# A hybrid decoder layer: gates spread over all partitions, sums of x and fourth-operand passes on POOL, attention weights merged ahead of the transpose

## The chip, the cores and the metric

The kernel runs on one core of one Trainium2 chip. The core's engines are TensorE (PE, with its weight loads as PEld), VectorE (DVE), ScalarE (ACT), GpSimd (POOL) and SyncE (SP, which here only issues DMAs). The metric is the device time of one launch in microseconds; the kernel before takes 2483.4 us, the median of three runs (2482.44 to 2484.32).

## The reference

One inference step of one layer: a projection of x (512 prompt rows and 8 x 4 sample rows, 2048 wide) to thirteen parts, an mLSTM branch and a sliding-window attention branch in parallel, a gated merge, an output projection and a layer norm. Everything is float32. What bears on the change:

```python
u = jnp.einsum('btd,dc->btc', x, w_in)          # parts: q_m k_m v_m o_m z_m q_a k_a v_a z_a g_m g_a i_pre f_pre
ig = i_pre + b_igate
lf = jax.nn.log_sigmoid(f_pre + b_fgate)         # 4 heads x 544 rows
...
dist = qi + WINDOW - kj                          # a block of 128 queries sees its own 128 keys and the 128 before
valid = (dist >= 0) & (dist < WINDOW) & ((blk > 0) | (kj >= WINDOW))
s = q @ k * hd ** -0.5 - slope[h] * dist         # 32 heads of 64, 4 key/value heads
p = softmax(concat([where(valid, s, -inf), sink]))[..., :-1]
out = p @ v
br_a = out * silu(z_a)
```

With a window of 128, a query at place i of its block sees the keys up to i in its own block and those beyond i in the block before: the two 128x128 blocks of weights are non-zero in opposite triangles (the own block with the diagonal).

## The kernel before

**Products.** Every product is made of three: operands are split into a high and a low part in fp32r (`hilo`, L243 to L245: ACT copies the high part, DVE subtracts it for the low part), and wh·xh, wh·xl and wl·xh are summed on PE. Weights come in by SP's DMAs as `raw` tiles of 128x1024, ACT casts `wh` (L200) and DVE subtracts for `wl` (L201).

**Seven products for eight.** The main part of the input projection takes two column tiles at a time (`paired`, L698, with `prepare`, `half_product` and `gather` from L638): a 2x2 split of weights and rows is multiplied with seven half products in place of eight. For this, sums of weight quarters are formed (L645 on DVE, or L643 as an accumulating DMA from POOL's queue), and four sums of x in tiles of 272 rows: `s1`, `n2`, `n3` and `s4`, each as a high and a low quad. `s1r`, `n2r` and `n3r` are their plain forms. A half product is 24 matmuls of 128x272 (L665 for the high weights, L667 for the low ones); its result goes to `ev` tiles by ACT (L683, L688), POOL (L684) and DVE (L686 to L694).

**The start.** x comes in by five DMAs on SP, PE transposes it (L321), ACT and DVE split it (L244, L245). For the first eight k tiles ACT also copies both halves out of PSUM into `n2r` and `s1r` (L328, L329, L339); for the others DVE subtracts (L333, L343); POOL forms `n3r` (L347). `x_sums` (L554 to L584) then makes the four operands: POOL subtracts for `n2r` (L557), `n3` is split first, then `s1` and `n2` behind the last piece of x, and once the plain products are done DVE makes the fourth operand in two passes for each of four chunks (L581, L582) and splits it. At the same time the two column tiles of V are multiplied (`gemm`, L595) and, between them, the gate columns (`gates_half`, L391).

**The gates.** `gates` (L394 to L522) works on rows of 4 partitions x 544: log-sigmoid of the forget gate by |f|, exp, a reciprocal (L421) and a series (to L433), then a running sum and maxima. `attn_values` (L524 on) transposes V and writes it out through `ev` tiles (a pool of three).

**Attention.** `attentions` (L856) goes through 16 pairs of heads as a generator; `tick()` after each half product takes it one step on, so its work stands in between the paired products. `attention` (L755 to L818) makes the scores of a head (L773), adds the slopes and takes the minimum on DVE (L775), exponentiates (L784) and scales by the sums (L790) on ACT; PE transposes seven blocks a head (L801, four own and three from the block before), they are split to `ph` and `pl` of 7x128 columns, and eight matmuls a head multiply them by V (L811). ACT, DVE and POOL finish `hT` (L814, L815, L817), SP stores it.

**Order.** The order of instructions on each engine is fixed when the kernel is built, by a scheduler that goes by priorities, buffers and `issue_after` constraints; on the chip each engine works through its list in order, waiting on semaphores. SP's and POOL's lists hold DMAs too, which wait in line like any instruction.

Of the kernel before, what the change touches and what calls it, by code (L numbers as in the profile page):

```python
# [74 lines left out]
def _build(tc, nc, i, o, es):  # L75
# [240 lines left out]
    for g in range(8):  # L316
        for q in range(2):
# [31 lines left out]
    t544 = pool(esG, "t544", 12)  # L349
# [44 lines left out]
    def gates(ps):  # L394
# [9 lines left out]
        ig, fg, u, u2 = row(), row(), row(), row()  # L404
        for p_, (u_, v_), (ig_, fg_) in zip(ps, *(
# [5 lines left out]
        V.tensor_scalar(fg, fg, bi[:, 1:2], None, op0=ALU.add)  # L411
        yield
        e_ = row()
        A.activation(e_, fg, AF.Abs)
        A.activation(e_, e_, AF.Exp, scale=-1.0)
# [3 lines left out]
        dd, s, s2, p, lf = row(), u, u2, row(), row()  # L419
        V.tensor_scalar(dd, e_, 2.0, None, op0=ALU.add)  # L420
        V.reciprocal(dd, dd)  # L421
        yield
        yield
        yield
        V.tensor_tensor(out=s, in0=e_, in1=dd, op=ALU.mult)
        V.tensor_tensor(out=s2, in0=s, in1=s, op=ALU.mult)
        yield
        V.tensor_scalar(p, s2, 1.0 / 15, None, op0=ALU.mult)
        for c in (13, 11, 9, 7, 5, 3):
            V.scalar_tensor_tensor(p, p, 1.0 / c, s2, op0=ALU.add, op1=ALU.mult)  # L430
            if c % 4 == 1:
                yield
        V.scalar_tensor_tensor(p, p, 1.0, s, op0=ALU.add, op1=ALU.mult)  # L433
        V.tensor_scalar(lf, fg, 0.0, None, op0=ALU.min)
        V.scalar_tensor_tensor(lf, p, -2.0, lf, op0=ALU.mult, op1=ALU.add)
        yield

        rst, c = s, s2
        V.memset(rst, 1.0)
        V.memset(rst[:, 0:SEQ:128], 0.0)  # L440
        V.memset(rst[:, SEQ:T:NTS], 0.0)
        V.tensor_tensor_scan(c, rst, lf, 0.0, ALU.mult, ALU.add)
        ap, d0 = lf, row()
        V.tensor_tensor(out=ap, in0=ig, in1=c, op=ALU.subtract)
        yield
        V.memset(d0, 0.0)
# [78 lines left out]
    def attn_values(kk, vt):  # L525
# [8 lines left out]
        vr, vs = ev(512), ev(128)  # L534
# [19 lines left out]
    def x_sums():  # L554
# [5 lines left out]
        for name, r_ in (("n3", n3r), ("s1", s1r), ("n2", n2r)):  # L560
            h_, l_ = S[name] = quad(act2, name)
            for ch in range(4):
                ks_ = two_k(ch)
                if name == "n3":
                    A.activation(h_[:, ks_], r_[:, ks_], AF.Copy, scale=-1.0)
                    V.scalar_tensor_tensor(l_[:, ks_], r_[:, ks_], -1.0, r32(h_[:, ks_]), op0=ALU.mult, op1=ALU.subtract)
                else:

                    with tc.issue_after(state["x_end"].ins):
                        hilo(r_[:, ks_], h_[:, ks_], l_[:, ks_])  # L570
                if ch % 2:
                    yield

        while not state.get("plain_done"):
            yield
        s4 = S["s4"] = quad(act, "s4")
        for ch in range(4):
            ks_ = two_k(ch)
            k0 = (ch * 2) % 4
            h12, l12 = (r32(xk2[p][ch // 2][:, k0:k0 + 2, 0:HT]) for p in range(2))  # L580
            V.tensor_tensor(out=n2r[:, ks_], in0=h12, in1=n2r[:, ks_], op=ALU.subtract)  # L581
            V.tensor_tensor(out=n2r[:, ks_], in0=n2r[:, ks_], in1=l12, op=ALU.add)  # L582
# [147 lines left out]
    def open_attention():  # L730
        for name, bufs in (("b1", 1), ("bs", 2), ("bt", 1), ("bq", 2), ("bm", 2)):
            bp[name] = pool(esB, name, bufs)

# [21 lines left out]
    def attention(k, qs, sz, kv):  # L755
# [5 lines left out]
        for a in range(2):  # L761
            nb = btile("b1", [128, 256], f"nb{a}")
# [1133 lines left out]
```

## Time and profile before

| | before |
|---|---|
| runs (median; lowest to highest) | 2483.4 us; 2482.44 to 2484.32 us |
| the profiled execution's time | 2483.67 us |
| its span | 2481.7 us |
| PE busy in the span | 2448.2 us |
| DVE, ACT, POOL busy | 1813.4, 1244.7, 372.7 us |

The profile is of one execution. Its page gives busy times, a chain of waits and groups of like instructions; the trace behind it can be asked for the time line of an engine, for the busy time in windows, for the waits of an engine with what ended them, and for groups by line and shape. Times are us from the start of the span. A name like `wl<-raw,wh` says what an instruction writes and reads.

### The profile page before, as it was taken

What the parts mean: (1) busy time and instruction counts of PE and PEld (TensorE: products, weight loads), DVE (VectorE), ACT (ScalarE), POOL (GpSimd) and SP (SyncE); (2) the same over time, 40 slices, a digit from 0 to 9 for tenths busy, and PEclk for the clock granted to TensorE, in tenths of its full rate; (3) what the DMA queues carried; (4) which work ended last, traced back from release to release, by engine and by line L of the source; (5) the groups of instructions that cost most, each with busy time, mean ns of one, the idle gap of its engine ahead of it and who ended that gap; (6) DMA issues with size and microseconds to landing.
All of it is one profiled execution on the core that took longest, in us unless ns stands there. A gap on an engine that the chain in (4) does not pass through costs nothing.

```text
span 2481.7 us, 48772 instructions
## 1 busy us (share of the span) xinstructions
PE 2448.2 (99%) x19542; PEld 2390.0 (96%) x19542; DVE 1813.4 (73%) x2785; ACT 1244.7 (50%) x2033; POOL 372.7 (15%) x376
## 2 busy tenths in 40 slices
PE   8999999999999999999999999999999999999997
PEld 8899999999999999999999999999999999999997
DVE  7867677677777777787877888887866654777667
ACT  6457677667667665353343444444633323434431
POOL 2111121111111111021111122211000000110101
PEclk9999999999999999999999999999999999999998
DMA  6676666666666655477677667587755546788776
GB/s 167 149 191 180 159 144 158 155 153 156 149 162 148 153 136 141 117 201 244 203 224 240 200 199 235 172 250 237 233 187 183 174 150 215 213 230 256 213 221 192
DMA packets 557172, 464.71 MB, mean 187 GB/s; under 512 B 45328, under 2 KB 454080, under 8 KB 556688
## 3 DMA queue, kind: packets, MB, share of 16 engines
q1 hardware_dynamic: 540048, 402.07, 54.4%
q0 software_dynamic: 15696, 57.15, 11.8%
q8 instruction: 154, 2.52, 0.4%
q10 hardware_dynamic: 1200, 2.36, 0.3%
q14 instruction: 74, 0.61, 0.1%
HBM read 319.06 MB, written 96.31 MB: 167 GB/s over the span
## 4 chain that ended last, share of the span: by engine, by line
PE 94%; DVE 2%; DMA 2%; ACT 1%; issue 0%; SPq 0%; POOL 0%; DVEq 0%; ACTq 0%; POOLq 0%
PE bank L665 45%; PE bank L667 22%; PE bank L210 13%; PE sm L1400 2%; PE bank L1212 1%; PE sm L1432 1%; PE sm L773 1%; PE sm L1445 1%; PE sm L811 1%; PE sm L210 1%; PE sm L801 1%; DMA raw<-in_w_in 1%; PE sm L1762 1%; PE sm L1217 1%; DVE wl L201 0%
## 5 line engine op out<-in xcount | busy, mean ns | idle before, releaser
L200 ACT CAST wh<-raw 128x1024 fp32r<-128x1024 f32 x632 | 661.9, 1048 | 806.6 <-PE bank L665 649.2
L201 DVE TENSOR_TENSOR wl<-raw,wh 128x1024 fp32r<-128x1024 f32 x632 | 776.4, 1230 | 229.6 <-ACT wh L200 202.8
L665 PE MATMUL bank<-xk,wh 128*128 128x272 f32 x2336 | 324.1, 289 | 1.9 <-DVE ev L690 1.9
L645 DVE TENSOR_TENSOR raw<-raw,raw 128x1024 f32<-128x1024 f32 x238 | 303.9, 1277 | 11.7 <-DMA raw<-in_w_in 3.6
L665 PEld LDWEIGHTS bank<-xk,wh 128*128 128x128 f32 x2336 | 303.1, 188 | 5.5 <-issue 2.6
L684 POOL TENSOR_TENSOR ev<-p,ev 128x272 f32<-128x272 f32 x82 | 123.8, 1509 | 638.5 <-ACT ev L683 590.5
L667 PE MATMUL bank<-xk,wl 128*128 128x272 f32 x1168 | 172.4, 288 | 0.8 <-DVE wl L201 0.8
L665 PE MATMUL bank<-s1h,wh 128*128 128x272 f32 x656 | 169.0, 291 | 0.1
L665 PE MATMUL bank<-n3h,wh 128*128 128x272 f32 x656 | 168.8, 289 | 0.1
L665 PE MATMUL bank<-s4h,wh 128*128 128x272 f32 x656 | 168.3, 290 | 0.1
L665 PE MATMUL bank<-n2h,wh 128*128 128x272 f32 x656 | 168.2, 289 | 0.0
L665 PE MATMUL bank<-n3l,wh 128*128 128x272 f32 x656 | 168.0, 287 | 0.0
L665 PE MATMUL bank<-n2l,wh 128*128 128x272 f32 x656 | 167.6, 287 | 0.0
L665 PE MATMUL bank<-s1l,wh 128*128 128x272 f32 x656 | 167.1, 287 | 0.0
L665 PE MATMUL bank<-s4l,wh 128*128 128x272 f32 x656 | 167.0, 287 | 0.0
L667 PEld LDWEIGHTS bank<-xk,wl 128*128 128x128 f32 x1168 | 156.5, 188 | 1.0 <-DVE wl L201 1.0
L665 PE MATMUL bank<-a11h,wh 128*128 128x272 f32 x584 | 150.6, 289 | 2.5 <-ACT wh L200 2.5
L665 PE MATMUL bank<-a11l,wh 128*128 128x272 f32 x584 | 149.8, 289 | 0.0
L210 PE MATMUL bank<-bh,wl 128*128 128x272 f32 x704 | 148.3, 289 | 0.0
L210 PE MATMUL bank<-bh,wh 128*128 128x272 f32 x704 | 148.1, 289 | 0.0
L210 PE MATMUL bank<-bl,wh 128*128 128x272 f32 x704 | 146.0, 288 | 0.9 <-DVE bl L245 0.9
L643 POOL DMA_DIRECT2D raw<-raw x90 | 77.8, 864 | 319.4 <-DVE sums L786 142.8
(487 smaller groups left out, 5554.9 us busy)
## 6 DMA issues: line engine op xcount, KB each, us to landing
raw<-in_w_in SPq DMA_DIRECT2D x296, 512.0 KB
raw<-raw POOLq DMA_DIRECT2D x90, 512.0 KB, 4.9
C<-in_state_mlstm_C SPq DMA_DIRECT2D x32, 1024.0 KB
out<-C SPq DMA_DIRECT2D x64, 512.0 KB
raw<-in_w_proj_a SPq DMA_DIRECT2D x32, 512.0 KB
raw<-in_w_proj_m SPq DMA_DIRECT2D x32, 512.0 KB
raw<-in_w_out SPq DMA_DIRECT2D x32, 512.0 KB
d_v<-ev SPq DMA_DIRECT2D x16, 272.0 KB
```

The costliest lines, as they stand in the source:

```text
L200: A.copy(wh[:, k:k + n], raw[:, k:k + n])
L201: state["split"] = V.tensor_tensor(out=wl[:, k:k + n], in0=raw[:, k:k + n], in1=r32(wh[:, k:k + n]), op=ALU.subtract)
L210: PE.matmul(ps[f][:, :w], a[:, kk], b(k, c, w), start=(k == 0 and n == 0), stop=(k == 15 and n == 2))
L643: G.dma_start(out=w[out][:], in_=w[b][:], accum_op=ALU.add)
L645: V.tensor_tensor(out=w[out][:], in0=w[a][:], in1=w[b][:], op=ALU.add)
L665: PE.matmul(ps, wh[:, k], x(p, k), start=(first and k == 0 and p == 0), stop=False, skip_group_check=True)
L667: state["end"] = PE.matmul(ps, wl[:, k], x(0, k), start=False, stop=(k == 7), skip_group_check=True)
L684: G.tensor_tensor(out=c22, in0=p1, in1=c11, op=ALU.subtract)
L773: PE.matmul(pp[:, c0 + w0:c0 + 256], qs[a][:, j * 128:j * 128 + 128], kx[:, k0:k0 + 256 - w0], start=(n == 0), stop=(n == 1))
L801: PE.transpose(pt[:, (m - m0_) * 128:(m - m0_) * 128 + 128], s_[:, b, 128:256] if own else s_[:, b + 1, 0:128], ident)
L811: PE.matmul(po[:, b * 128:b * 128 + n], VA[:, b], p_[:, 2 * b:2 * b + n // 128], start=(b == 0 and m == 0), stop=(b == 3 and m == 1), skip ...
L1400: PE.matmul(pp[:, 0:258], a[:, b * 128:b * 128 + 128], b_[:, b, f], start=(b == 0 and n == 0), stop=(b == 3 and n == 2))
```

## The change

It has five parts; numbers and order of PE's other work stay.

1. **Sums of x.** For the first eight k tiles the plain `n2r` and `s1r` are no longer copied out of PSUM by ACT, but added on POOL from the high and low halves after they are split, two k tiles at once. In `x_sums` all three splits stand behind the last piece of x, and `s1` comes ahead of `n3`.
2. **Fourth operand.** Its two passes for each of the four chunks go from DVE to POOL, ahead of the wait for the plain products.
3. **Gates.** The biased forget gate row (4x544) goes by a DMA to 17 columns on all partitions; the log-sigmoid is made there, and a second DMA takes it back to 4x544. Three memsets move to POOL.
4. **V's tail tile** in `attn_values` comes from the pool of gate rows (13 buffers, was 12) and no longer from `ev`.
5. **Attention weights.** After the exponentials POOL adds the block before to the own block (three blocks of four have one); ACT scales only the merged 128 columns; PE transposes four blocks a head; ACT copies them to `fh`, DVE subtracts for `fl`; then POOL from `fh` and DVE from `fl` multiply by a mask `upper` (the exponential of the triangle constant) for the own parts and subtract for the parts of the block before, into tiles `P` of 7x128 as before. Both heads' tiles are made ahead of the matmuls with V; the pool holds three of them, and one step of the generator is moved.

```diff
             if k < 8:
                 hilo(pt[:, 0:HT], a11[0][:, k], a11[1][:, k])
                 hilo(pt[:, HT:SEQ], a21[0][:, k, 0:SEQ - HT], a21[1][:, k, 0:SEQ - HT])
-                A.copy(n2r[:, k], pt[:, 0:HT])
-                A.copy(s1r[:, k, 0:SEQ - HT], pt[:, HT:SEQ])
...
                 hilo(src, *(a21[p][:, k4, SEQ - HT:HT] for p in range(2)))
-                A.copy(s1r[:, k4, SEQ - HT:HT], src)
+                for t_, (h_, l_) in ((s1r, a21), (n2r, a11)):
+                    for ch in (g - 1, g):
+                        ks_ = two_k(ch)
+                        G.tensor_tensor(out=t_[:, ks_], in0=r32(h_[:, ks_]), in1=r32(l_[:, ks_]), op=ALU.add)
...
-    t544 = pool(esG, "t544", 12)
+    t544 = pool(esG, "t544", 13)
...
+        w7 = t5(n=6 * 17)
...
-        e_ = row()
-        A.activation(e_, fg, AF.Abs)
-        A.activation(e_, e_, AF.Exp, scale=-1.0)
...
-        V.tensor_scalar(dd, e_, 2.0, None, op0=ALU.add)
-        V.reciprocal(dd, dd)
...
-        V.tensor_scalar(lf, fg, 0.0, None, op0=ALU.min)
-        V.scalar_tensor_tensor(lf, p, -2.0, lf, op0=ALU.mult, op1=ALU.add)
...
+        f7, e7, d7, s7, q7, p7 = (w7[:, n * 17:n * 17 + 17] for n in range(6))
+        nc.sync.dma_start(f7, fg)
+        yield
+        yield
+        A.activation(e7, f7, AF.Abs)
+        A.activation(e7, e7, AF.Exp, scale=-1.0)
+        yield
+        V.tensor_scalar(d7, e7, 2.0, None, op0=ALU.add)
+        V.reciprocal(d7, d7)
...
+        V.scalar_tensor_tensor(f7, p7, -2.0, f7, op0=ALU.mult, op1=ALU.add)
+        nc.sync.dma_start(lf, f7)
+        G.memset(rst, 1.0)
+        G.memset(rst[:, 0:SEQ:128], 0.0)
+        G.memset(rst[:, SEQ:T:NTS], 0.0)
...
-        vr, vs = ev(512), ev(128)
+        vr, vs = ev(512), t5(n=128)
...
-        for name, r_ in (("n3", n3r), ("s1", s1r), ("n2", n2r)):
+        for name, r_ in (("s1", s1r), ("n3", n3r), ("n2", n2r)):
...
-            V.tensor_tensor(out=n2r[:, ks_], in0=h12, in1=n2r[:, ks_], op=ALU.subtract)
-            V.tensor_tensor(out=n2r[:, ks_], in0=n2r[:, ks_], in1=l12, op=ALU.add)
+            G.tensor_tensor(out=n2r[:, ks_], in0=h12, in1=n2r[:, ks_], op=ALU.subtract)
+            G.tensor_tensor(out=n2r[:, ks_], in0=n2r[:, ks_], in1=l12, op=ALU.add)
+        while not state.get("plain_done"):
+            yield
...
-        for name, bufs in (("b1", 1), ("bs", 2), ("bt", 1), ("bq", 2), ("bm", 2)):
+        for name, bufs in (("b1", 1), ("bs", 2), ("bt", 3), ("bq", 2), ("bm", 2)):
...
+        A.activation(upper[:], cc[:, C_TRI:C_TRI + 128], AF.Exp)
...
+            G.tensor_tensor(out=s_[:, 1:4, 128:256], in0=s_[:, 1:4, 0:128], in1=s_[:, 1:4, 128:256], op=ALU.add)
...
-                sj = s_[:, j, 128 if j == 0 else 0:256]
+                sj = s_[:, j, 128:256]
                 A.activation(sj, sj, AF.Copy, scale=sums[:, j:j + 1])
...
-            ph, pl = (btile("bt", [128, 7, 128], t_, F32R) for t_ in ("ph", "pl"))
-            for m0_, m1_ in ((0, 4), (4, 7)):
-                pt = sm()
-                for m in range(m0_, m1_):
-                    b, own = m // 2, m % 2 == 0
-                    PE.transpose(pt[:, (m - m0_) * 128:(m - m0_) * 128 + 128],
-                                 s_[:, b, 128:256] if own else s_[:, b + 1, 0:128], ident)
-                n = m1_ - m0_
-                hilo(blk(pt[:, 0:n * 128], n), ph[:, m0_:m1_], pl[:, m0_:m1_])
-            yield
+            pt = sm()
+            for b in range(4):
+                PE.transpose(pt[:, b * 128:b * 128 + 128], s_[:, b, 128:256], ident)
+            fh, fl = s_[:, :, 0:128], s_[:, :, 128:256]
+            A.copy(fh.bitcast(F32R), blk(pt[:]))
+            V.tensor_tensor(out=fl.bitcast(F32R), in0=blk(pt[:]), in1=fh, op=ALU.subtract)
+            up = bp["upper"][:].unsqueeze(1).to_broadcast([128, 4, 128])
+            both = []
+            for e, f in ((G, fh), (V, fl)):
+                p_ = btile("bt", [128, 7, 128], "P", F32R)
+                e.tensor_tensor(out=p_[:, 0:7:2], in0=f, in1=up, op=ALU.mult)
+                e.tensor_tensor(out=p_[:, 1:7:2], in0=f[:, 1:4], in1=r32(p_[:, 2:7:2]), op=ALU.subtract)
+                both.append(p_)
+            ps_.append(both)
+            yield
+        for a in range(2):
             yield
             po = sm()
...
-                for m, p_ in enumerate((ph, pl)):
+                for m, p_ in enumerate(ps_[a]):
...
-        yield
+            if a == 0:
+                yield
```

More of the change, by code (lines that the diff above doesn't have):

```diff
@@ L421, in gates @@
-        V.reciprocal(dd, dd)
+        A.activation(e7, f7, AF.Abs)
[3 more added lines that the diff above has]
+        V.reciprocal(d7, d7)
+        V.tensor_tensor(out=s7, in0=e7, in1=d7, op=ALU.mult)
+        V.tensor_tensor(out=q7, in0=s7, in1=s7, op=ALU.mult)
+        V.tensor_scalar(p7, q7, 1.0 / 15, None, op0=ALU.mult)
+        for n in (13, 11, 9, 7, 5, 3):
+            V.scalar_tensor_tensor(p7, p7, 1.0 / n, q7, op0=ALU.add, op1=ALU.mult)
@@ L422, in gates @@
+        V.scalar_tensor_tensor(p7, p7, 1.0, s7, op0=ALU.add, op1=ALU.mult)
+        V.tensor_scalar(f7, f7, 0.0, None, op0=ALU.min)
+        V.scalar_tensor_tensor(f7, p7, -2.0, f7, op0=ALU.mult, op1=ALU.add)
[3 more added lines that the diff above has]
+        G.memset(rst[:, SEQ:T:NTS], 0.0)
         yield
         yield
-        yield
-        V.tensor_tensor(out=s, in0=e_, in1=dd, op=ALU.mult)
-        V.tensor_tensor(out=s2, in0=s, in1=s, op=ALU.mult)
@@ L427, in gates @@
[L427 to L433, printed above, removed]
-        V.tensor_scalar(lf, fg, 0.0, None, op0=ALU.min)
-        V.scalar_tensor_tensor(lf, p, -2.0, lf, op0=ALU.mult, op1=ALU.add)
-        yield
-        rst, c = s, s2
-        V.memset(rst, 1.0)
@@ L563, in x_sums @@
                 ks_ = two_k(ch)
[L564 to L569, printed above, removed]
+                with tc.issue_after(state["x_end"].ins):
+                    if name == "n3":
+                        A.activation(h_[:, ks_], r_[:, ks_], AF.Copy, scale=-1.0)
+                        V.scalar_tensor_tensor(l_[:, ks_], r_[:, ks_], -1.0, r32(h_[:, ks_]), op0=ALU.mult,
+                                               op1=ALU.subtract)
+                    else:
                         hilo(r_[:, ks_], h_[:, ks_], l_[:, ks_])
```

20 lines of the change are left out of this document (11 added, 9 removed).

## The prediction

> **What bounds the kernel now.** I read the page's first part and its chain of waits, then PE's waits over the whole run, then the engines' busy time in windows: ten-microsecond ones at the start, and the sixteen periods of attention (141 to 960 us). In a window row the figures after the window's length are busy us of PE, PEld, DVE, ACT and POOL, then granted clock, DMA share and GB/s; a sum row speaks for itself.
>
> ```profile
> PE 2448.2 (99%) x19542; PEld 2390.0 (96%) x19542; DVE 1813.4 (73%) x2785; ACT 1244.7 (50%) x2033; POOL 372.7 (15%) x376
> PE 94%; DVE 2%; DMA 2%; ACT 1%; issue 0%; SPq 0%; POOL 0%; DVEq 0%; ACTq 0%; POOLq 0%
> 473.00:520.00 47.00, 47.00 (x382) 47.00 (x381) 33.65 (x54) 33.01 (x61) 8.85 (x7) 1.00 0.62 151
> sum 819.00, PE 818.33 PEld 817.59 DVE 592.54 ACT 552.65 POOL 145.12; mean PE 48.14 PEld 48.09 DVE 34.86 ACT 32.51 POOL 8.54
> 10.00:20.00 10.00, 8.03 (x41) 6.99 (x42) 5.96 (x14) 7.90 (x25) 1.34 (x1) 0.83 1.09 360
> 20.00:30.00 10.00, 9.00 (x64) 7.70 (x65) 8.39 (x18) 9.25 (x30) 6.11 (x5) 1.00 0.37 38
> 30.00:40.00 10.00, 9.45 (x77) 9.24 (x77) 8.33 (x16) 6.50 (x12) 4.24 (x4) 1.00 0.66 169
> 40.00:50.00 10.00, 9.29 (x75) 9.04 (x75) 9.90 (x17) 4.17 (x10) 3.54 (x3) 1.00 0.28 72
> 50.00:60.00 10.00, 10.00 (x82) 10.00 (x82) 9.96 (x17) 6.60 (x12) 1.01 (x1) 1.00 0.69 165
> ```
>
> PE is busy for 2448.2 of 2481.7 us and holds 94% of the chain: only PE work removed, or PE idle time made or closed, moves the end. In the attention PE is full (0.67 us idle in 819), while DVE, ACT and POOL have 13, 14 and 38 us of room in a period of 47. At the start it is otherwise: PE idles 2.97 us between 10 and 30, and between 40 and 60 DVE is full (19.86 of 20). So the change has to be judged in two places with opposite limits.
>
> **Term 1: transposes in the attention.** Each of 32 heads drops from seven 128x128 transposes to four; 96 go, and the PV matmuls stay at 8 per head. PE's timeline gives the price (start, us, engine, line, operation, and in brackets the idle time before with its releaser): seven transposes, then the start of what follows them. The last row is their group, with count, busy us and mean ns.
>
> ```profile
> 483.62 0.92 PE L801 MATMUL sm<-cc,s 128*128 128x128 f32 x7
> 484.31 0.37 PE L665 MATMUL bank<-s1h,wh 128*128 128x272 f32 x1
> 491.27 0.95 PE L801 MATMUL sm<-cc,s 128*128 128x128 f32 x7
> 491.97 2.26 PE L665 MATMUL bank<-xk,wh 128*128 128x272 f32 x16
> L801 PE MATMUL sm<-cc,s 128*128 128x128 f32 x224 | 30.0, 274 | 0.0
> ```
>
> 484.31 less 483.62 is 0.69, 491.97 less 491.27 is 0.70: 0.0986 us a transpose in the stream. The group's busy time, 30.0/224 = 0.134, holds overlap with neighbours and is the upper bound. 96 x 0.0986 = 9.5 us saved (at most 12.9). I take 9.5, since starts in a full stream are what the end follows.
>
> **What must cover it.** The split tiles that PV reads are now made after the transposes from the four merged blocks, and most of that is POOL's. Per head: an add of 128x3x128 ahead of the transposes, a product 128x4x128 and a difference 128x3x128 on POOL; product and difference also on DVE. POOL's prices come from the nearest rows (the second L1193 row has shortest, median and longest ns).
>
> ```profile
> 30.17 1.36 POOL L557 TENSOR_TENSOR n2r<-n2r,r 128x544 f32<-128x544 f32 x1
> L817 POOL TENSOR_TENSOR hT<-sz,hT 128x512 f32<-128x512 f32 x16 | 36.3, 2268 | 165.3 <-issue 154.9 <-DVE hT L815 10.4
> L1193 POOL TENSOR_SCALAR Ab<-KB,cc 128x128 fp32r<-128x128 f32 x32 | 33.5, 1046 | 186.7 <-DMA KB<-d_kv 149.9 <-PE bank L665 18.8 <-PE sm L1217 18.1
> L1193 POOL TENSOR_SCALAR Ab<-KB,cc x32: 603/792/2392, 1069.7 to 1710.1; 128x128 fp32r<-128x128 f32 x32
> 484.26 0.97 ACT L244 CAST ph<-sm 128x512 fp32r<-128x512 f32 x2
> 488.06 1.45 POOL L684 TENSOR_TENSOR ev<-p,ev 128x272 f32<-128x272 f32 x1 [9.20 <-ACT ev L683]
> 489.47 0.86 POOL L643 DMA_DIRECT2D raw<-raw  x1
> raw<-raw POOLq DMA_DIRECT2D x90, 512.0 KB, 4.9
> ```
>
> Low price, by elements from 1.36 for 544: product 1.28, difference and add 0.96 each, 6.4 us per period of two heads. Middle, from L817's 2.27 for 512 (beside a busy DVE): 2.27 and 1.70, 11.3 us. High, from L1193, POOL's only row with an fp32r output, four and three times 1.05: product 4.2, difference 3.1, 14.6 for these and 1.9 to 3.4 for the adds. Added to 8.85 this leaves POOL at 15 to 27 of 47 us: it isn't the bound, its order is.
>
> That order, from the first head's four transposes (time 0): product and difference of head 0, L684's add, product of head 1, an accumulating weight DMA, difference of head 1. PE runs on with 24 matmuls, four transposes, 48 matmuls, PV of head 0, 48 matmuls, PV of head 1. Between 484.31 and 491.27 stand 48 matmuls and a PV: 6.96. So PV of head 0 is due near 9.8, PV of head 1 near 16.8, and the accumulated weights must be cast by 16.5 to feed the matmuls at 17.6. With ACT's copy (some 0.6, at about 0.4) POOL starts at 1.0. At the middle price: 3.3, 5.0, 6.5 (the add 1.45), 8.7, DMA issued 9.6, landed 14.5 (4.9), difference of head 1 at 11.3. All in time by 2 us or more. At the high price the first P is ready at 8.3, still in time, but the DMA lands at 1.0+4.2+3.1+1.45+4.2+0.86+4.9 = 19.7, 3.2 late. I take the middle: no stall, 0 us; the far end goes to a rival. What ACT and DVE gain or lose here (64 casts and 64 subtractions for 32 copies and 96 operations) is hidden by their 13 us of room. With three buffers for four P tiles, DVE's tile of head 1 waits for PV of head 0, done at 10.6, and DVE's next lower-weight pass stands behind it; that one is due at 19.6 (the matmuls of 17.6 and their first 16), so 0 again.
>
> **Term 2: the start.** It gives and takes. The x sums leave ACT (18 copies) for eight POOL adds that read the split halves; the fourth operand's eight passes go from DVE to POOL; the log-sigmoid works on 17 columns of 128 partitions instead of 544 of 4, for two small DMAs; a copy of V no longer waits for an `ev` slot. The two DMAs stand in SP's queue among weight loads, and SP waits there for DVE:
>
> ```profile
> SPq L187 <- DVE wl L201: 276.1, 82, 9.2
> 69.68 1.26 PE L667 MATMUL bank<-xk,wl 128*128 128x272 f32 x8 [0.80 <-DVE wl L201]
> 78.30 0.39 PE L665 MATMUL bank<-a11h,wh 128*128 128x272 f32 x1 [0.81 <-ACT wh L200]
> 82.47 2.28 PE L665 MATMUL bank<-xk,wh 128*128 128x272 f32 x16 [1.92 <-DVE ev L690]
> 104.74 0.39 PE L665 MATMUL bank<-a11h,wh 128*128 128x272 f32 x1 [1.73 <-ACT wh L200]
> 65.01 3.54 DVE L421 RECIPROCAL t<-t 4x544 f32<-4x544 f32 x1
> 73.24 6.65 DMA out<-ev
> 80.02 0.28 DVE L536 COPY ev<-sm 32x128 f32<-32x128 f32 x1 [3.83 <-DMA out<-ev]
> 91.99 3.84 DMA d_ks<-ev
> ```
>
> Gains: the wait at 69.68 follows the long reciprocal, which goes; those at 78.30 and 82.47 follow DVE's 3.83 us stop at 80.02, which was for the `ev` slot, and go too: 0.80 + 0.81 + 1.92 = 3.5. The 1.73 at 104.74 hangs on a weight DMA through POOL's queue that the change doesn't touch. ACT, 9.25 of 10 busy at 20 to 30, is lighter; I allow 0.5. SP's new waits (a DMA that stands until the gate row is ready) hold back loads behind them; SP waits 276 us in the run for buffers to come free (82 waits, first row) and PE isn't held by it, so 0. Bound on this side: -4.0.
>
> Losses: POOL now has ten more passes of 128x544 in a stretch where DVE is full.
>
> ```profile
> 40.13 3.78 DVE L245 TENSOR_TENSOR s1l<-r,s1h 128x544 fp32r<-128x544 f32 x4
> 44.01 2.63 DVE L245 TENSOR_TENSOR n2l<-n2r,n2h 128x544 fp32r<-128x544 f32 x4
> 40.36 1.70 POOL L557 TENSOR_TENSOR n2r<-n2r,r 128x544 f32<-128x544 f32 x1 [3.37 <-DVE r L333]
> 47.40 1.99 DVE L581 TENSOR_TENSOR n2r<-xk,n2r 128x544 f32<-128x544 f32 x3
> 60.93 0.49 DVE L411 TENSOR_SCALAR t<-t,bi 4x544 f32<-4x544 f32 x1
> ```
>
> The same four DVE passes take 3.78 beside one POOL pass and 2.63 without, and that POOL pass takes 1.70, not 1.36: the two engines delay each other by nearly a whole pass. POOL's passes from n2 on to the fourth operand (1.36 each, 13.6 us) now stand among some 16 us of DVE passes with two SBUF operands. If they only ever alternate, the forget gate's bias add (60.93 before) comes near 66, though 5.3 us of L581 and L582 have left DVE (eight of 0.66, by the 47.40 row). Behind it ACT, which works in order, holds its absolute value until the small DMA has landed (3.84, as at 91.99), and the cast of the weights for n2 is queued behind. Walked along the new orders with these durations (PE's work for x itself up to 1.7 us earlier than before, out of the 2.97 us that it idles at 10 to 30), PE idles 3.8 us ahead of the second half of the V columns (their lower weights stand behind n3's passes on DVE), 2.2 ahead of s1 and 3.6 ahead of n2, and reaches the matmuls of 82.47 at 85.6: +3.1, the three waits gone included. Bounds -4.0 and +3.1; I take +1.5, nearer to the alternating end because the 40.13 row shows it happening.
>
> [...]
>
> **Term 3: the rest.** From some 990 us on the order on every engine is the same as before, and the tail after PE's last matmul too: 0.
>
> **Sum**, against the profiled execution's own time (2483.67, span 2481.7, 2.0 around it, and 0.3 above the median of the three runs, 2483.4): 2483.67 - 9.5 + 1.5 = **2475.7 us**. A change within 0.2%, some 5 us, can't be told from none in this kernel, so 2478.4 to 2488.4 is "the same".
>
> **The rivals.**
> - *The start alternates fully*, as the 40.13 row has it for one pass, for all ten: 2483.67 - 9.5 + 3.1 = 2477.3. For it: the 40.13 row; against: between its passes POOL waits for its own inputs, and a pass that finds DVE reading PSUM runs freely. 0.20.
> - *The start only gains*: DVE's load falls by 5.3 us of passes and the reciprocal's 3.5, ACT's by 18 copies, so that all three waits go and POOL keeps up: 2483.67 - 9.5 - 4.0 = 2470.2. Against: POOL passes of 1.36 replace DVE ones of 0.66 on the same dependent chain. 0.12.
> - *The gates' round trip decides*: the DMA of the gate row takes 6.65 as the row at 73.24, not 3.84; ACT stands 2.8 longer ahead of a cast which PE needs. With the full alternation: 2477.3 + 2.8 = 2480.1, the same. For it: 128 pieces of 17 columns are smaller than what 91.99 moved. 0.12.
> - *POOL late in the attention* (the slower side): fp32r outputs cost as L1193's mean, the accumulating DMA lands 3.2 late in every period, PE waits ahead of the matmuls of 17.6: 2475.7 + 16 x 3.2 = 2526.9. It decides from 2.0 us of POOL lateness beyond the middle price; at 0.6 us of PE wait a period 9.6 us are lost and the gain is gone. For it: no row prices such an output at this size; against: L1193's median is 0.79 and its shortest 0.60, by which (product 2.4, difference 1.8) the DMA lands at 14.9, in time. 0.11.
> - My own forecast has the other 0.45.
>
> **How the numbers follow.** Low end: 2483.67 - 12.9 - 4.0 = 2466.8. High end: round trip 2480.1, and POOL with a third of a microsecond late per period, 2480.1 + 5.3 = 2485.4, rounded to 2486. Outside lie most of the POOL case and little else. Faster: 0.45 + 0.12 + two thirds of the 0.20 and the round trip's small share, 0.70. Slower: the POOL case, 0.11. The same: 0.19.
>
> **What would show it.** PE's count falls by 96; the transposes stand in fours of about 0.4 us; the attention windows stay full and a period falls by 0.59 us (9.5/16). A PE wait there on P or on the cast behind the accumulating DMA is the POOL case. At the start, a wait of the second-half V matmuls on `wl` near 40 us and of s1 and n2 on `wh` between 60 and 72 confirms the alternation; no waits there and none near 70 to 82 is the pure gain. The whole is wrong if a new wait comes up after 990 us, where I changed nothing.

## The result, and the profile after

The changed kernel takes 2476.13 us, the median of eight runs (2473.57 to 2479.48), against 2483.53 for eight runs of the kernel before (2481.28 to 2485.48): a ratio of 0.9972, with a 95% interval of 0.9961 to 0.9983, so 7.4 us faster (4 to 10). Its profiled execution took 2477.29 us, 1.2 above that median.

First the page (busy times, chain by engine), then windows of the changed kernel, in the columns of before, with the sums over 0 to 140 and over the attention's windows.

```profile
PE 2441.1 (99%) x19446; PEld 2383.9 (96%) x19446; DVE 1877.4 (76%) x2805; ACT 1215.2 (49%) x1984; POOL 531.7 (21%) x492
PE 89%; DMA 4%; DVE 3%; POOL 1%; issue 1%; ACT 0%; SPq 0%; DVEq 0%; POOLq 0%; ACTq 0%
```

```profile
60.00:70.00 10.00, 6.28 (x34) 5.73 (x33) 6.94 (x14) 4.88 (x10) 2.97 (x6) 0.69 0.47 106
70.00:80.00 10.00, 10.00 (x68) 9.99 (x68) 5.23 (x12) 3.48 (x5) 3.31 (x4) 0.80 0.49 108
sum 140.00, PE 125.38 PEld 122.08 DVE 98.37 ACT 64.93 POOL 54.96; mean PE 11.40 PEld 11.10 DVE 8.94 ACT 5.90 POOL 5.00
473.00:520.00 47.00, 47.00 (x381) 47.00 (x380) 38.95 (x58) 31.92 (x61) 17.09 (x13) 1.00 0.65 155
sum 819.00, PE 817.51 PEld 816.42 DVE 670.75 ACT 532.06 POOL 285.05; mean PE 48.09 PEld 48.02 DVE 39.46 ACT 31.30 POOL 16.77
```

PE's count is down by the 96 transposes. POOL's work in the attention has doubled (285 us in 819), and PE is still full in every window of it but the last, 899 to 960, where it idles 1.49 us (0.67 before). At the start something new stands: between 60 and 80 us PE idles 3.7 us, and the granted clock is 0.69 and 0.80 where it was 1.00 before.

Two places give the account. In the attention, PE's timeline of the changed kernel, then two rows of before: the first transposes of the attention, and those 47 us later than the first row that the prediction quoted:

```profile
202.70 0.60 PE L802 MATMUL sm<-cc,s 128*128 128x128 f32 x4
483.02 0.60 PE L802 MATMUL sm<-cc,s 128*128 128x128 f32 x4
483.38 0.37 PE L666 MATMUL bank<-s1h,wh 128*128 128x272 f32 x1
529.76 0.60 PE L802 MATMUL sm<-cc,s 128*128 128x128 f32 x4
```

```profile
199.44 0.93 PE L801 MATMUL sm<-cc,s 128*128 128x128 f32 x7
530.99 0.92 PE L801 MATMUL sm<-cc,s 128*128 128x128 f32 x7
```

A period was 530.99 - 483.62 = 47.37 and is 529.76 - 483.02 = 46.74: 0.63 us less, 10.1 in sixteen. The first transposes come 3.3 us later than before, with as many matmuls ahead of them (1426 in either trace): so much the start lost in this execution. The last matmul of the run starts 6.1 us earlier (2459.08 in place of 2465.17), and one right behind the attention's samples at 1016.13 in place of 1021.93, 5.8 earlier. The 6.1 is 0.7 short of 10.1 - 3.3; about as much goes in the last window, where PE now waits 1.04 us at 943.15 for a DMA of the old keys, a wait that the kernel before doesn't have. By the medians 10.1 - 7.4 = 2.7 are lost in both places together.

One trace fixes the start's loss only roughly: attn_only (below), whose start is that of before, reaches its first transposes at 197.77, and both_pool, whose start is that of the changed kernel, at 199.95. Two executions of one start are 1.7 and 2.8 us apart.

At the start PE's order is not quite that of before: V's transposes (L530) and the gate columns now stand in the middle of V's second column tile. These are PE's longer waits for weights from 35 us on, in the changed kernel:

```profile
41.93 0.39 PE L210 MATMUL sm<-a11h,wl 128*128 128x272 f32 x1 [0.64 <-DVE wl L201]
62.80 0.39 PE L666 MATMUL bank<-s1h,wh 128*128 128x272 f32 x1 [1.78 <-ACT wh L200]
67.96 0.59 PE L666 MATMUL bank<-n2h,wh 128*128 128x272 f32 x1 [1.94 <-ACT wh L200]
95.73 0.39 PE L666 MATMUL bank<-n2h,wh 128*128 128x272 f32 x1 [1.00 <-ACT wh L200]
```

Of the waits of before between 69 and 105 us (5.26) three are gone and the fourth has shrunk from 1.73 to 0.25 (at 108.28), and those of these rows are there instead. What PE's clock does between them is read from two-microsecond windows, of which one is shown, and from the distance of two neighbouring matmuls:

```profile
64.00:66.00 2.00, 2.00 (x9) 1.69 (x8) 2.00 (x3) 0.00 (x0) 0.00 (x0) 0.50 0.75 135
63.28 0.28 PE L666 MATMUL bank<-s1l,wh 128*128 128x272 f32 x1
63.41 0.29 PE L666 MATMUL bank<-s1h,wh 128*128 128x272 f32 x1
64.45 0.43 PE L666 MATMUL bank<-s1h,wh 128*128 128x272 f32 x1
64.68 0.43 PE L666 MATMUL bank<-s1l,wh 128*128 128x272 f32 x1
```

At 63.3 us a matmul starts every 0.13 us, at 64.5 every 0.23: the clock is halved from about 63.7 to 74 (the window from 74 on has 1.00 again). In the five windows from 64 to 74 PE was busy for 8.06 us; at half clock 45% of that is loss ((0.227 - 0.125)/0.227), 3.6 us. Before had this for its first 140 us:

```profile
sum 140.00, PE 126.17 PEld 121.45 DVE 108.93 ACT 70.75 POOL 31.30; mean PE 11.47 PEld 11.04 DVE 9.90 ACT 6.43 POOL 2.85
```

PE idled 13.8 us in it then and 14.6 now: the waits have moved. Up to the first transposes PE is idle 0.8 us more and busy 2.5 us more (188.08 in place of 185.62) for the same number of matmuls: most of the 3.3 us is the clock.

### The profile page after: what moved, and what is told of

Its sections match the earlier page's. It is cut to its first block, busy times and chain, and to the rows that moved or that the text cites. A ratio compares the mean times of both kernels' runs of the same rounds, so it can differ in the third digit from the quotient of the medians.

```text
span 2475.4 us, 48813 instructions
## 1 busy us (share of the span) xinstructions
PE 2441.1 (99%) x19446; PEld 2383.9 (96%) x19446; DVE 1877.4 (76%) x2805; ACT 1215.2 (49%) x1984; POOL 531.7 (21%) x492
## 3 DMA queue, kind: packets, MB, share of 16 engines
q10 hardware_dynamic: 1200, 2.36, 0.3%
## 4 chain that ended last, share of the span: by engine, by line
PE 89%; DMA 4%; DVE 3%; POOL 1%; issue 1%; ACT 0%; SPq 0%; DVEq 0%; POOLq 0%; ACTq 0%
PE bank L666 45%; PE bank L668 22%; PE bank L210 10%; PE sm L1412 2%; PE bank L1224 1%; PE sm L1444 1%; PE sm L776 1%; PE sm L1457 1%; PE sm L822 1%; DMA tx<-d_y 1%; DMA ty<-d_y 1%; PE sm L1774 1%; DMA raw<-in_w_in 1%; DVE wl L201 1%; PE sm L802 1%
## 5 line engine op out<-in xcount | busy, mean ns | idle before, releaser
L201 DVE TENSOR_TENSOR wl<-raw,wh 128x1024 fp32r<-128x1024 f32 x632 | 790.7, 1252 | 210.6 <-ACT wh L200 184.2
L685 POOL TENSOR_TENSOR ev<-p,ev 128x272 f32<-128x272 f32 x82 | 118.0, 1439 | 442.0 <-ACT ev L684 419.4
```

Source lines behind the costliest of these rows:

```text
L201: state["split"] = V.tensor_tensor(out=wl[:, k:k + n], in0=raw[:, k:k + n], in1=r32(wh[:, k:k + n]), op=ALU.subtract)
L685: G.tensor_tensor(out=c22, in0=p1, in1=c11, op=ALU.subtract)
```

## The experiments

### The attention alone, and the rest alone

attn_only puts the fifth part alone on the kernel before; start_only is the changed kernel with the attention of before.

Against the kernel before and the changed kernel in turn:

```diff
-        for name, bufs in (("b1", 1), ("bs", 2), ("bt", 1), ("bq", 2), ("bm", 2)):
+        for name, bufs in (("b1", 1), ("bs", 2), ("bt", 3), ("bq", 2), ("bm", 2)):
...
-                PE.transpose(pt[:, (m - m0_) * 128:(m - m0_) * 128 + 128],
-                             s_[:, b, 128:256] if own else s_[:, b + 1, 0:128], ident)
+                PE.transpose(pt[:, b * 128:b * 128 + 128], s_[:, b, 128:256], ident)
...
```

```diff
-        for name, bufs in (("b1", 1), ("bs", 2), ("bt", 3), ("bq", 2), ("bm", 2)):
+        for name, bufs in (("b1", 1), ("bs", 2), ("bt", 1), ("bq", 2), ("bm", 2)):
...
-                PE.transpose(pt[:, b * 128:b * 128 + 128], s_[:, b, 128:256], ident)
+                PE.transpose(pt[:, (m - m0_) * 128:(m - m0_) * 128 + 128],
+                             s_[:, b, 128:256] if own else s_[:, b + 1, 0:128], ident)
...
```

> The kernel before with the change's fifth part alone (attention weights merged, three P buffers). My theory: all of the gain is here, 96 transposes at 0.0986 us, 9.5 us: 2483.5 - 9.5 = 2474.0, the first transposes of the attention at 199.4 us as before, a period 0.59 us shorter, PE full in the attention windows. Rival, each transpose worth its busy time (0.134): 2483.5 - 12.9 = 2470.6. Rival, the gain came from the start: 2483.5 within 1 us.

> The changed kernel with the attention of before: parts one to four alone. My theory: the start costs, as the first transposes of the attention come at 202.7 us in the changed kernel's trace against 199.4 before: 2483.5 + 3.3 = 2486.8 where the clock falls to 0.50 for some 10 us after PE's waits at 62.8 and 68.0 us, about 2483 where it doesn't. Rival, the start gains as much as its three removed waits: 2480.0.

Measured: attn_only 2474.55 us (ratio 0.9966, 0.9954 to 0.9979), 8.5 below the 2483.03 of before in the same comparison; start_only 2485.81 (1.0010, 1.0001 to 1.0018), 2.8 above. The gain is the attention's, and parts one to four together cost, though the interval of that cost is wide (0.2 to 4.5 us). start_only's profile shows the same place: a wait of 3.02 us for the weights of n2 at 67.23, and behind it a granted clock of 0.59 between 68 and 72 us.

### Two things in ACT's queue

Why does PE wait at 62.80 and 67.96? These are rows of ACT, SP and DVE in the changed kernel:

```profile
61.16 0.64 ACT L244 CAST s4h<-n2r 128x544 fp32r<-128x544 f32 x1 [1.14 <-POOL n2r L578]
61.71 1.04 ACT L200 CAST wh<-raw 128x1024 fp32r<-128x1024 f32 x1
63.47 0.67 SPq L418 DMA_DIRECT2D t<-t  x1
66.50 0.22 ACT L421 ACTIVATE t<-t 128x17 f32<-128x17 f32 x1 [3.06 <-DMA t<-t]
66.88 1.03 ACT L200 CAST wh<-raw 128x1024 fp32r<-128x1024 f32 x1
62.92 0.48 DVE L413 TENSOR_SCALAR t<-t,bi 4x544 f32<-4x544 f32 x1
```

ACT waits for POOL's fourth-operand passes with four casts (the last at 61.16), ahead of the weight cast for s1 (61.71); then for the gate's small DMA, ahead of the cast for n2 (66.88). That DMA goes out behind DVE's bias add at 62.92. s4_late holds the fourth operand's split behind the casts of n2; s4_gates_late holds the gates' absolute value back too.

```diff
+        s4 = S["s4"]                      # its own generator, spawned ahead of the paired products
         for ch in range(4):
             ks_ = two_k(ch)
-            hilo(n2r[:, ks_], s4[0][:, ks_], s4[1][:, ks_])
-            yield
+            with tc.issue_after(state["wh"].ins), tc.issue_after(state["split"].ins):
+                hilo(n2r[:, ks_], s4[0][:, ks_], s4[1][:, ks_])
+            if ch % 2:
+                yield
...
-        A.activation(e7, f7, AF.Abs)      # s4_gates_late
+        with tc.issue_after(state["wh"].ins):
+            A.activation(e7, f7, AF.Abs)
```

> The changed kernel, with the split of the fourth operand held behind the weight casts of n2 (ACT) and the lower weights of n2 (DVE). My theory: the casts of the fourth operand's high parts, which wait for POOL's passes, stand in ACT's queue ahead of the weight cast for s1 and make PE wait 1.78 us; DVE's low parts stand ahead of the forget gate's bias, so the gate's small DMA comes 6 us late and ACT's absolute value makes PE wait another 1.94; the clock drops to 0.50 behind these two waits and costs some 3.7 us (a matmul of 272 columns each 0.227 us in place of 0.125). All three go: 2476.1 - 1.8 - 1.9 - 3.7 = 2468.7, no PE wait between 58 and 75. Rival, the clock falls anyhow (or the waits only move on): 2472.4 to 2476.

> As the run before it, and the gates' absolute value held behind the weight cast of n2 as well. My theory: the same 2468.7, as the small DMA has landed by then in either. Rival, the round trip of the gate row is a wait of its own: this one is 2 us faster than the run before it.

Measured: s4_late 2476.92 us (0.9977, 0.9968 to 0.9986), no gain; s4_gates_late 2471.18 (0.9953, 0.9940 to 0.9965), each of its five runs (2469.81 to 2472.53) below each of the changed kernel's eight. My theory missed for the first, where the waits moved on, and was 2.5 us short for the second; there the rival held that the round trip of the gate row is a wait of its own, by 5.7 us between the two runs and not by 2. Rows of s4_late, PE and DVE:

```profile
68.05 0.39 PE L672 MATMUL bank<-n2h,wh 128*128 128x272 f32 x1 [2.93 <-ACT wh L200]
60.99 0.07 DVE L447 MEMSET t<- 4x8 f32 x1 [3.09 <-POOL t L416]
61.04 0.49 DVE L413 TENSOR_SCALAR t<-t,bi 4x544 f32<-4x544 f32 x1
```

With nothing of the fourth operand ahead of it, the bias add still came at 61.04, though DVE was free from 57.9. Between the two stands DVE's small memset of the row d0 (60.99), which waits 3.09 us for POOL's memset of the same row; that one stands in POOL's queue behind all eight passes. In the changed kernel the row is this:

```profile
55.68 5.44 POOL L578 TENSOR_TENSOR n2r<-n2r,xk 128x544 f32<-128x544 f32 x3
61.06 0.54 POOL L416 MEMSET t<- 4x544 f32 x1
```

### The memset back on DVE

```diff
-        G.memset(d0, 0.0)
+        V.memset(d0, 0.0)
```

> The run s4_late (fourth operand's split held back, 2476.9) with one memset, that of the row d0, back on DVE. What s4_late showed: the gate's bias add on DVE came at 61.04 although DVE was free from 57.9, as DVE's small memset of the same row ahead of it waits for POOL's memset, which stands in POOL's queue behind all eight fourth-operand passes. My theory: with the memset on DVE the bias add comes near 58, the small DMA lands near 63 at the latest, PE's wait of 2.93 at 68 shrinks under 0.5 and the clock doesn't fall behind it: 2476.9 - 2.5 - 2 = 2472.4, near s4_gates_late (2471.2). Rival, the gate's DMA is slow in itself or held in SP's queue: the wait stays, 2476.9.

> The run s4_gates_late (2471.2) with the memset of d0 back on DVE. My theory: there the waits in question were gone already, so 2471.2 within 1 us; the gates only come some 2 us earlier, which may take the wait of 1.64 at 95.6 us for an ev tile: 2469.5 at best. Rival, the memset's 4x544 on DVE costs as much in front of the lower weights: 2472.

Measured: s4_late_d0 2475.96 us (0.9976, 0.9966 to 0.9986); best, which is s4_gates_late with this edit, 2470.78 (0.9956, 0.9944 to 0.9969), as s4_gates_late and as forecast. The first forecast failed on the time and held only for the wait in question: in s4_late_d0 PE has no wait between 43 and 73 us. The bias add moved only to 60.26, as everything on DVE was later in this execution (the lower weights ahead of it stand at 59.03, in s4_late at 56.04), but it follows them at once. The execution also has a wait of 4.31 us for lower weights at 42.65, where s4_late's had 0.64. What came later on is in its DVE and PE rows:

```profile
81.06 1.28 DVE L442 TENSOR_TENSOR_SCAN t<-t,t 4x544 f32<-4x544 f32 x1 [4.77 <-DMA t<-t]
82.82 2.53 PE L672 MATMUL bank<-xk,wh 128*128 128x272 f32 x15 [3.33 <-DVE ev L697]
```

The second DMA of the gates' round trip takes 5.1 us from its issue at 75.87; DVE waits for it in order, and an `ev` result that frees a bank for PE stands behind. Either leg held an engine that had other work: ACT for 3.06 us at 66.50 in the changed kernel, DVE for 4.77 here.

### Which engine holds the start

> The changed kernel with its second part undone (the fourth operand's eight passes on DVE, behind the plain products, as before). My theory: the eight passes on POOL are what costs at the start. DVE takes 5.3 us of passes back but loses the delay beside POOL (lower weights 2.04 and 1.85 in place of 1.2, the weight sum 2.38, the first low part 1.88: 3.8 us), so PE's waits of 1.78 and 1.94 and the clock's 3.7 go: 2476.1 - 7.4 = 2468.7. Rival, DVE is the bound there whoever makes the passes: the waits stay, 2476 to 2478.

> The run best (2470.8) with the splits of the x sums held on DVE behind the first lower weights of V's second column tile. What best showed: PE waited 4.31 us for these at 42.37, as DVE's four passes for n3's low part stand ahead of them and took 4.91 beside POOL's passes (2.62 in the changed kernel's profile), and the clock fell to 0.50 behind that wait (0.69 on the mean of 40 to 50). My theory: the lower weights come at 36 to 37, the wait falls under 1 us and the clock stays, so 2470.8 - 3.5 - 2.5 = 2464.8 in executions like that one, 2467 on the median. Rival, DVE beside POOL is the bound whatever the order, and the wait moves to the next lower weights or the gate columns: 2470 to 2471.

fourth_dve undoes part two; best2 holds the x sums' splits in best behind the first lower weights of V's second column tile.

```diff
-            G.tensor_tensor(out=n2r[:, ks_], in0=h12, in1=n2r[:, ks_], op=ALU.subtract)
-            G.tensor_tensor(out=n2r[:, ks_], in0=n2r[:, ks_], in1=l12, op=ALU.add)
         while not state.get("plain_done"):
             yield
...
+            V.tensor_tensor(out=n2r[:, ks_], in0=h12, in1=n2r[:, ks_], op=ALU.subtract)
+            V.tensor_tensor(out=n2r[:, ks_], in0=n2r[:, ks_], in1=l12, op=ALU.add)
             hilo(n2r[:, ks_], s4[0][:, ks_], s4[1][:, ks_])
```

```diff
+        first = state["split"]            # at the head of x_sums
...
-                with tc.issue_after(state["x_end"].ins):
+                with tc.issue_after(state["x_end"].ins), tc.issue_after(first.ins):
```

Measured: fourth_dve 2474.05 us (0.9967, 0.9955 to 0.9980), 2 us below the changed kernel, where 7 were expected, and not settled against its 0.9972 (0.9961 to 0.9983); best2 2470.63 (0.9951, 0.9939 to 0.9964), as best, so here the rival held. Rows of best (DVE, PE) first, then of best2 (PE):

```profile
36.27 4.91 DVE L567 SCALAR_TENSOR_TENSOR n3l<-r,n3h 128x544 fp32r<-128x544 f32 x4
42.37 0.60 PE L210 MATMUL sm<-a11h,wl 128*128 128x272 f32 x1 [4.31 <-DVE wl L201]
```

```profile
39.32 0.39 PE L210 MATMUL sm<-a11h,wl 128*128 128x272 f32 x1 [0.27 <-DVE wl L201]
47.04 0.49 PE L392 MATMUL bank<-xk,wga 128*128 128x272 f32 x2 [1.61 <-DVE wga L387]
54.09 0.68 PE L210 MATMUL sm<-xk,wl 128*128 128x272 f32 x2 [2.28 <-DVE wl L201]
```

best2 brings the wait at V's second half from 4.31 to 0.27 and gets 1.61 and 2.28 further on. In fourth_dve POOL is out of the way from 45 us, DVE's passes from there on take their short time again (0.65 us in each of three groups of four, 1.21 for the lower weights at 52.07), the waits for s1 and n2 and the halved clock are gone, and DVE's own extra 5.2 us make PE wait 1.29 at 53.33 and 1.02 at 78.72. So with the passes on either engine DVE has too much there (19.92 of 20 us busy from 40 to 60 in both runs); in these runs the order only chose who waits.

### The other parts undone

gates_old undoes part three, sums_act part one as far as ACT's copies go, best3 is best with those copies.

```diff
-        nc.sync.dma_start(f7, fg)
...
-        V.reciprocal(d7, d7)
...
-        nc.sync.dma_start(lf, f7)
+        e_ = row()
+        A.activation(e_, fg, AF.Abs)
...
+        V.reciprocal(dd, dd)
...
```

```diff
-                for t_, (h_, l_) in ((s1r, a21), (n2r, a11)):
+                A.copy(n2r[:, k], pt[:, 0:HT])
+                A.copy(s1r[:, k, 0:SEQ - HT], pt[:, HT:SEQ])
```

> The changed kernel with its third part undone (log-sigmoid on 4 x 544, no small DMAs, memsets on DVE). My theory: the round trip of the gate row costs at this place what the long reciprocal cost before: the wait of 1.94 at 68 goes with half of the clock's loss, a wait of some 0.8 for lower weights behind the reciprocal (3.54) comes back: 2476.1 - 1.9 - 1.8 + 0.8 = 2473.2. Rival, spreading the gates is a gain of its own and undoing it costs: 2477 to 2479.

> The changed kernel with its first part undone as far as the plain sums go (ACT copies them out of PSUM again; eight POOL adds fall away). My theory: these adds end by 28 us, ahead of the stretch where POOL and DVE hold each other up, so little hangs on them: 2476.1 within 1.5. Rival, they push POOL's later passes into DVE's full stretch: 2472 to 2473. Rival, ACT, 9.25 of 10 us busy between 20 and 30 in the kernel before, is the bound there: 2478.

> The run best (2470.8: fourth operand's split and the gates' absolute value held back, the memset of d0 on DVE) with the plain sums by ACT again as in sums_act, where PE stood full from 30 to 50 us, and lost 2.16 at 52.5 (lower weights), 3.19 at 66.5 (DVE behind POOL's memset) and some 4 by the clock after that. My theory: with eight POOL adds less the early waits for DVE go (PE's first wait is the one at 52.5), and the two holds and the memset's place take the 3.19 and the clock's loss away: 2477.5 - 3.2 - 4 = 2470.3, and 2469 if the 2.16 shrinks. Rival, POOL's eight fourth-operand passes beside DVE set the end of the start whatever comes before them, so that the earlier idle time only moves behind them: 2470.8 as best. Rival, the low parts and the sums come later on DVE: 2473.

Measured: gates_old 2474.58 us (0.9966, 0.9953 to 0.9978), sums_act 2477.48 (0.9979, 0.9970 to 0.9988), best3 2472.41 (0.9956, 0.9943 to 0.9970). Against the changed kernel's 0.9972 neither of the first two is settled: gates_old is 1.6 us faster, where 2.9 were forecast, and sums_act 1.4 slower, inside the 1.5 that were allowed. best3 can't be told from best; of its forecasts, too near to each other to be parted by the time, the profile fits the rival: with a start that is full to 47 us PE waits 2.14 at 49.49 and 1.37 at 61.62 instead.

### The slack of the attention

```diff
-            for e, f in ((G, fh), (V, fl)):
+            for e, f in ((G, fh), (G, fl)):
```

> The changed kernel with both P tiles of a head made on POOL (the low half's product and difference move from DVE). It measures the slack of the attention. By the changed kernel's trace (products 1.87, differences 1.43 on average; first product at 1.6 us after the first transposes; accumulating DMA to cast 5.4 us; PE needs that cast by 17.7 and the second head's tiles by 16.9): the DMA is issued 3.4 us later, cast done at 17.7, the last tile at 17.1. My theory: PE waits 0.2 to 0.9 us in each of 16 periods, on P or on that cast: 2476.1 + 3 to 14. Rival, the slack is larger: 2476. Rival, POOL's operations with fp32r outputs get as slow as the 1.05 us for 128 columns elsewhere: 3 us late a period, 2524.

Measured: 2480.67 us (0.9991, 0.9982 to 1.0000), 4.5 above the changed kernel, inside the 3 to 14 of my theory, but with other waits than it had. POOL's rows of the changed kernel, whose period starts with the transposes at 483.02, and then rows of both_pool, whose period starts at 482.12:

```profile
484.59 1.56 POOL L811 TENSOR_TENSOR P<-s,upper 128x512 fp32r<-128x512 f32 x1 [5.55 <-ACT s L804]
486.23 1.34 POOL L812 TENSOR_TENSOR P<-s,P 128x384 fp32r<-128x384 f32 x1
490.80 0.86 POOL L644 DMA_DIRECT2D raw<-raw  x1
```

```profile
482.12 0.60 PE L802 MATMUL sm<-cc,s 128*128 128x128 f32 x4
484.42 3.79 POOL L811 TENSOR_TENSOR P<-s,upper 128x512 fp32r<-128x512 f32 x2 [5.55 <-ACT s L804]
488.17 2.00 POOL L812 TENSOR_TENSOR P<-s,P 128x384 fp32r<-128x384 f32 x2
491.85 1.29 POOL L811 TENSOR_TENSOR P<-s,upper 128x512 fp32r<-128x512 f32 x1
493.08 0.85 POOL L644 DMA_DIRECT2D raw<-raw  x1
498.36 2.00 ACT L200 CAST wh<-raw 128x1024 fp32r<-128x1024 f32 x2 [4.67 <-DMA raw<-raw]
366.72 1.27 PE L668 MATMUL bank<-s1h,wl 128*128 128x272 f32 x8 [0.43 <-DVE wl L201]
```

Counted from the transposes, the DMA went out 11.0 us on in place of 7.8, 3.2 later where 3.4 were forecast, and the cast behind it starts at 16.2 in place of 13.2. PE waits neither for a P tile nor for that cast; the last two products take 1.29 us and the last difference 1.01 (at 491.85, 495.05 and 496.42), where the changed kernel has 1.87 and 1.43 on average. But ACT stood 4.67 us for the DMA, and DVE, which waits for ACT's cast, 2.76 (to 499.44); what it makes after that, lower weights and q, comes late in some periods, and there PE waits 0.2 to 0.5 us at a time. That DVE's backlog is the cause was read from this one period and not tested. PE idles 2.07 us between 200 and 800 (windows of 200 us show 0 for the changed kernel). The one of 0.43 cost more than its idle time: two starts are 0.72 us apart (366.00 to 366.72) in place of 0.125. From the first to the last pair's transposes 705.12 us go by (199.95 to 905.07), in the changed kernel 700.84 (202.70 to 903.54): 4.3 us more, so nearly all of the 4.5 is in the attention.

## Why the prediction was right

The forecast was 2475.7 and the median is 2476.1, 0.4 off, and 1.6 off the profiled execution; its two terms were each a little too small, and these errors took opposite sides. That it came so near is in part luck: the eight runs spread over 5.9 us, and their interval holds the rival of the full alternation, 2477.3, as well.

- **PE sets the end**: right. The removed PE work and the start's waits and clock moved it, and 0.8 us of waits in the last window of the attention, which the sum did not have; from 1016 us to the last matmul the two traces keep their distance within 0.3 us.
- **The transposes, -9.5**: right in mechanism and nearly in size. Measured 0.63 us a period in place of 0.59, 10.1 in all, between the 9.5 taken and its upper bound of 12.9. attn_only alone gives 8.5, with an interval of 5 to 11.
- **The attention's cover**: right. The middle prices for POOL were 2.27 and 1.70, the groups of the changed kernel have 1.87 and 1.43:

```profile
L811 POOL TENSOR_TENSOR P<-s,upper 128x512 fp32r<-128x512 f32 x32 | 59.9, 1870 | 88.3 <-ACT s L804 88.3
L812 POOL TENSOR_TENSOR P<-s,P 128x384 fp32r<-128x384 f32 x32 | 45.8, 1430 | 1.3
492.93 1.04 PE L822 MATMUL sm<-P,VA 128*128 128x256 f32 x8
496.25 1.05 ACT L200 CAST wh<-raw 128x1024 fp32r<-128x1024 f32 x1 [1.65 <-DMA raw<-raw]
```

  PV of the first head starts 9.9 us after the first transposes (forecast 9.8), with P ready at 4.6; the cast behind the accumulating DMA runs at 13.2, due by 16.5. So the rival of a late POOL was 3 us away, which both_pool used up, and POOL's fp32r outputs (1.87 us for 512 columns) are no dearer here than its fp32 ones (2.27 for 512 in the kernel before).
- **The start, +1.5 between -4.0 and +3.1**: the term that was mis-sized, as far as it can be told. It measures +2.8 in start_only (0.2 to 4.5), at most 2.7 by the medians, and 3.3 in the profiled execution: nearer to the bound of the full alternation than to what I took, but the interval holds both.

  The gains came, but not all for the reasons that I gave: the three waits went, and the fourth (1.73), which I left in place, shrank to 0.25, with 1.00 new in its stead at 95.73. The wait at 82.47 does follow DVE's stop for the `ev` slot: in attn_only, with the start of before, the stop is 2.82 us in place of 3.83 and the wait 0.81 in place of 1.92. The wait at 78.30 does not: in the trace of before its cast starts on ACT at 76.25, when DVE's stop has just begun. And in gates_old, where V's copy no longer waits for a slot, PE still waits 1.84 us at 81.57, as DVE stands 1.79 for a cast there.

  The three new waits were at the places named, with 0.64 (4.3 in other executions with the same order up to there), 1.78 and 1.94 in place of 3.8, 2.2 and 3.6. What the step lacked is the clock: 3.6 us behind waits that I had priced at their length only. So shorter waits than forecast and an unpriced clock came to about the forecast's upper bound, and not the alternation as I had walked it. And it had the reason of the last two incomplete: the memset that moved to POOL, which the sum did not price at all, holds DVE's bias add (at 62.92, forecast near 66) behind POOL's passes.
- **The round trip of the gate row**: the first leg took 3.0 us (63.47 to 66.50), not 3.84, so the rival with 6.65 did not come about in the changed kernel; the second leg of 5.1 us that made PE wait in s4_late_d0 was on no list.
- **No gain shown from the spread gates and the moved sums**: the rival in which the start only gains (2470.2) came near only with two holds in ACT's queue that the change doesn't have: s4_gates_late, 2471.2, and best, 2470.8.

## What to carry to other kernels

Where PE is full, price a removed PE instruction by the distance of starts in the stream and believe it (0.59 us a period forecast, 0.63 measured); what has to be watched is the queue of each helper engine, since here four casts and an absolute value, each short in itself and standing ahead of two weight casts, cost 5 us (2476.1 against 2471.2). Before work is moved from DVE to POOL, list the DVE passes that will run beside it: the fourth operand's eight passes took 5.2 us on DVE in fourth_dve and 15.7 on POOL in the changed kernel (45.43 to 61.12). And price a new wait of PE with the clock's loss that can follow it, not only with its own length: 3.4 us at half clock cost a full PE some 1.5 us here, by an estimate from the two distances of starts (45% of 3.4).

## What the runs showed of the hardware

Beside POOL passes over SBUF tiles, DVE instructions with two SBUF inputs took up to some seven times as long here as without them (2.06 us against 0.28 for two of 32 columns). Rows of DVE and POOL in the changed kernel, then the same two DVE instructions in best:

```profile
31.50 2.06 DVE L387 TENSOR_TENSOR wga<-graw,wga 128x32 fp32r<-128x32 f32 x2
30.85 2.67 POOL L556 TENSOR_TENSOR n2r<-n2r,r 128x544 f32<-128x544 f32 x2
39.51 2.36 DVE L201 TENSOR_TENSOR wl<-raw,wh 128x1024 fp32r<-128x1024 f32 x1
```

```profile
29.66 0.28 DVE L387 TENSOR_TENSOR wga<-graw,wga 128x32 fp32r<-128x32 f32 x2
41.10 1.21 DVE L201 TENSOR_TENSOR wl<-raw,wh 128x1024 fp32r<-128x1024 f32 x1
```

Two instructions of 32 columns take 2.06 us beside two POOL passes and 0.28 without (in best a POOL memset runs beside them), a weight pass 2.36 and 1.21. In both cases POOL's pass had begun first (30.85 ahead of 31.50, and one at 39.42 ahead of 39.51). A POOL pass beside which DVE read the PSUM tile `sm` kept its short time, 1.37 us, in the kernel before:

```profile
32.63 1.37 POOL L557 TENSOR_TENSOR n2r<-n2r,r 128x544 f32<-128x544 f32 x1 [1.11 <-DVE r L333]
32.80 0.67 DVE L245 TENSOR_TENSOR xk<-sm,xk 128x512 fp32r<-128x512 f32 x1
33.40 0.39 DVE L333 TENSOR_TENSOR r<-sm,r 128x240 f32<-128x240 f32 x1
```

Who came first differed between executions: in best POOL's two passes began at 36.19, ahead of DVE's four for n3's low part at 36.27, which took 4.91 us; in the changed kernel's profile these began at 36.97, ahead of POOL's at 39.42, and took 2.62. With one order of instructions the wait ahead of V's second half was 0.64 us in the changed kernel's profile and 4.29 in both_pool's, whose start is the same.

The clock was halved, to 0.50, at or behind PE waits that add up to 1.6 to 4.3 us within some four microseconds (1.64 in s4_gates_late, 1.78 in the changed kernel, 2.28 in best2, 3.33 in s4_late_d0). Others of 1.92 (before, at 82.47), 2.16 (sums_act, at 52.52) and 2.14 (best3, at 49.49) passed at 1.00. Three waits ahead of V's second half, 1.68 us in all, halved it in start_only, and the same three, 1.70 us, did not in the changed kernel. So neither the length alone nor the place in the program decided it in these runs. How long it lasted is more regular. Matmuls started every 0.125 us or every 0.227; with the clock taken as full or half accordingly, a window of w us with granted clock c had 2 x w x (1 - c) us at half clock. Summed over a stretch this estimate gives 3.4 us in best2, s4_late and s4_gates_late (twice each in the last two; the second of s4_gates_late is read from its matmuls, 0.23 us apart from 96.22 on), 6.8 in best, both_pool and sums_act, and 10.2 in the changed kernel, where a second wait fell into it: one, two or three times 3.4. What sets the 3.4 us, and which waits bring it on, no run here shows.
